# Layer 1's down phase: output rows on GpSimd's queue, other leads for loads and residual rows, weight sums from the third period

## The chip, the core and the metric

The kernel runs on one core of a Trainium2 chip. The metric is the device time of one execution in microseconds (us); the median of the runs counts. The core has a matrix engine (TensorE, PE in the profile), a vector engine (VectorE, DVE), an activation engine (ScalarE, ACT), GpSimd (POOL) and SyncE (SP), which only issues transfers. All of them run their own instructions in program order and wait for each other through semaphores. Transfers (DMA) between the main memory and the on-chip memory are issued here by SP and by POOL. PE writes its sums to banks (PSUM), from which VectorE and ScalarE read.

## What is computed

The reference is a small diffusion backbone with two layers over 1024 latent tokens of width 1024 and 256 context tokens. Each layer has attention and a feed-forward network with a short convolution, each followed by a residual sum and a layer norm:

```
        f_lat = conv_ffn(modulate(x_lat, m_lat[3], m_lat[4]), ffn_w_up[l], ffn_conv_w[l], ffn_conv_b[l], ffn_w_down[l])
        x_lat = layer_norm(DN_ALPHA * x_lat + m_lat[5] * f_lat, ln_g[l, 1], ln_b[l, 1])
...
def conv_ffn(h, w_up, conv_w, conv_b, w_down):
    u = h @ w_up
    L = u.shape[1]
    r = CONV_W // 2
    up = jnp.pad(u, ((0, 0), (r, r), (0, 0)))
    acc = conv_b
    for j in range(CONV_W):
        acc = acc + up[:, j:j + L] * conv_w[j]
    a, g = jnp.split(acc, 2, axis=-1)
    return (jax.nn.silu(g) * a) @ w_down
```

Here `w_up` is 1024 x 5632 and `w_down` 2816 x 1024. The second layer (number 1) returns only the latent rows, so its last layer norm gives the output: 1024 rows of 1024 floats.

## The kernel before

Everything is float32 at the boundary. For PE each operand is split in two parts, a rounded one (a cast on ScalarE) and the remainder (a subtraction on VectorE), and each block product is three matmuls. `split` (L101) does this for tiles of 128x512: the cast is L112, the subtraction L113.

The change lies in `ffn7` (L2070), layer 1's feed-forward network, and in `finish_o` in `run`, its last layer norm. Both matrix products there are done with seven block products in place of eight, with sums of blocks made beforehand. All engines run in the order in which the code is written (`manual_schedule`), so the place of a line in the program is its place in each engine's queue.

**Up phase.** 22 periods `p`, one for each pair of 128-column blocks of the up weights. Each has seven products on PE (L1691; 12 matmuls each). ScalarE copies banks and makes casts (L1663), VectorE subtracts and sums weights (L1665 to L1670), applies the convolution (L2149) and multiplies with the gate (L2181); the results and sums of them go to a buffer `G` in main memory through POOL's queue (L2155). The weights of period `p + 2` are loaded in period `p` (L1644).

Beside it runs the generator `side` = `mix_down` (L2037): for each of 11 rows of blocks of the down weights it loads four blocks of 128x512 on SP (L2046), makes four differences on VectorE (L2050) and stores them to a buffer `V` through POOL (L2051). It yields seven times a row, 77 times in all, and is advanced by `next(side, None)` at four places in each period. What is left is run after the last period. In the last period `load(0)` is issued near the start, and `load(1)` after it.

**Down phase.** 77 steps, 11 for each of seven products `q`; a step is 12 matmuls (L2350), three for each of four blocks of 128 rows. The sums lie in two groups of four banks, X and Y (`dx` and `dy` in the profile); `banks` says which product uses which. Between products ScalarE copies one group to the other (`copies`, L2390, after steps 10, 21, 43 and 65), and VectorE evicts finished banks to the rows `z` (`evict`: L2360 to L2365, also L2362 and L2363 where a saved part is added). `end` (L2371) finishes a row: statistics (L357 on VectorE, L359 and L360 on POOL), two passes over the row (L2809, L2812), and the store to the output (L2813 on SP).

`load(j)` (L2110) brings what steps 2j and 2j+1 need: a pair of weight blocks (from `V`, L2120, or from the down weights) and a pair from `G` (L2121), both 512 KB, on SP; then casts (L112 twice, L2129 for the `G` part) and subtractions (L113 twice, L2130). Each takes two of six raw buffers (`fr`), and of the split tiles there is room for six loads. Ahead of the steps of an even `i`, all loads up to `n` that were not yet issued are written: `n` is the step's own load plus a lead.

`job(i, ...)` hangs work behind step `i`: the loads of the residual rows z (L2394) and of the norm's and gate's rows, the scaling of the rows (`scale`, L2368 and L2369), `begin` (two rows for the last norm), the copies, evictions and ends. The jobs of rows 0 to 3 (`evict` with the saved part at steps 55, 57, 59, 61, `end` at 56, 58, 60, 62) fall between loads 33 to 36. The last nine steps run row block by row block: for each of the blocks 4 to 7 nine steps, then its eviction and its end.

Of the kernel before, what the change touches and what calls it, by code (L numbers as in the profile page):

```python
# [37 lines left out]
class Kern:  # L38
# [2031 lines left out]
    def ffn7(self, l, B, hps, T, dT, xsrc, gate_row, view, begin, finish, norm,  # L2070
# [3 lines left out]
        nc, io, d = self.nc, self.io, self.d  # L2074
# [5 lines left out]
        with ExitStack() as es:  # L2080
# [29 lines left out]
            def load(j):  # L2110

                s, m = 2 * j, min(2, 7 * HF - 2 * j)
                if m <= 0:
                    return
                r, g = raw(), raw()
                if m == 2 and (s + 1) % HF == 0:
                    nc.sync.dma_start(r[:, :1], right(s, 1))
                    nc.sync.dma_start(r[:, 1:], right(s + 1, 1))
                else:
                    nc.sync.dma_start(r[:, :m], right(s, m))  # L2120
                nc.sync.dma_start(g[:, :m], Gv[:, s : s + m])  # L2121
                for i, w in enumerate(self.split([r[:, i] for i in range(m)], 512)):
                    wd[s + i] = w
                if j < 3:
                    for i, w in enumerate(self.split([g[:, i] for i in range(m)], 512)):
                        ga[s + i] = w
                    return
                w = self.t(gp[0], [128, 2, 2, 512], "w", R)
                nc.scalar.copy(w[:, 0, :m], g[:, :m])  # L2129
                nc.vector.tensor_sub(w[:, 1, :m], g[:, :m], f32(w[:, 0, :m]))  # L2130
                for i in range(m):
                    ga[s + i] = w[:, :, i]

            side = self.mix_down(up, l)
# [80 lines left out]
            def get_T(m):  # L2215
                if m in more:
                    T[m], make[m] = self.load_T(tp, stage(m), dT, m, 0)

            def make_T(m, *which):
                if m in make:  # L2220
                    make[m](*which or range(3))

            c = none()
            late_l, YQ = None, {}

            def adds(Y, Q):


                for ps in (Y, Q):
                    nc.tensor.matmul(ps, ah[:, 0, :128], ah[:, 0], start=True, stop=True)  # L2230

            with self.tc.manual_schedule(engines=every):
                for m in range(4):
                    if m == 2 and 0 in make:
                        make_T(0)
                        make_T(1)
                    get_T(m)
                    for p in pre if m == 1 else []:
                        X, Y, Q = YQ[p] = (early["x", p],) + tuple(
                            self.t(pu, [128, 512], f"{x}{p}") for x in "yq"  # L2240
                        )
                        adds(Y, Q)
                        nc.scalar.copy(Y, X)
                        self.product(early[p][0][2], b21, X, False)
                for p in range(NP):
                    W2, call = [], lambda *x: None
                    if p == 0 and pre:
                        W2, call0 = early[1]
                        call = lambda what, i: i in (0, 2) or call0(what, i)
                    elif p + 1 < NP:  # L2250
                        W2, call = self.up_parts(raws)
                    if p in pre:
                        X, Y, Q = YQ[p]
                    else:
                        X = self.t(px or pu, [128, 512], f"x{p % 2}")
                        Y, Q = (self.t(pu, [128, 512], f"{x}{p % 2}") for x in "yq")
                    V = self.t(pu, [128, 512], f"v{p % 2}")
                    if p < 2 and p not in pre:
                        adds(Y, Q)
                    ua = self.t(up, [128, TLAT], "ua", bufs=2)  # L2260
                    ug = self.t(up, [128, TLAT], "ug")
                    u0, u1, v0, v1 = (view(u, h) for u in (ua, ug) for h in range(2))
                    if p not in pre:
                        self.product(W[0], (ah, al), X, True)
                    if late_l:
                        late_l("l", 5)
                        late_l("l", 6)
                    if p not in pre:
                        nc.scalar.copy(Y, X)
                    if p == NP - 1:  # L2270
                        load(0)
                    call("s", 1)
                    call("h", 0)
                    c.a1()
                    self.product(W[1], T[0], V, True)
                    if p + 2 < NP:
                        raws = self.up_raws(l, ORDER[p + 2])
                    nc.scalar.copy(u1, cols(V))
                    if p == 0:
                        make_T(2)  # L2280
                    call("h", 1)
                    c.g1()
                    call("l", 0)
                    c.a2()
                    next(side, None)
                    self.product(W[4], T[1], Y, False)
                    nc.scalar.copy(Q, Y)
                    if p == 0:
                        make_T(3)
                    call("h", 2)  # L2290
                    call("l", 1)
                    c.g2()
                    next(side, None)
                    if p not in pre:
                        self.product(W[2], b21, X, False)
                    nc.scalar.copy(u0, cols(X))
                    c.silu()
                    call("h", 3)
                    call("s", 4)
                    call("l", 2)  # L2300
                    self.product(W[5], T[2], Q, False)
                    call("h", 4)
                    call("l", 3)
                    c.store()
                    nc.vector.tensor_tensor(v1, u1, cols(Q), ALU.add)  # L2305
                    next(side, None)
                    self.product(W[6], b22, Y, False)
                    call("l", 4)
                    call("s", 5)
                    call("s", 6)  # L2310
                    nc.vector.tensor_tensor(u1, u1, cols(Y), ALU.add)
                    self.product(W[3], T[3], Q, False)
                    nc.scalar.copy(v0, cols(Q))
                    call("h", 5)
                    call("h", 6)
                    c.mix()
                    next(side, None)
                    c = conv(ua, ug, p)
                    W, late_l = W2, call
                for _ in side:  # L2320
                    pass
                load(1)
                for x in (c.a1, c.g1, c.a2, c.g2, c.silu, c.store, c.mix):
                    x()
# [3 lines left out]
        with ExitStack() as es, self.tc.manual_schedule(engines=every):  # L2328
            zp = es.enter_context(self.pool("fz"))
            gp[0] = es.enter_context(self.pool("fgs", bufs=6))  # L2330
            pd = es.enter_context(self.pool("fd", space=PSUM))
            z = [self.t(zp, [128, D], f"z{t}") for t in range(NLAT)]
# [43 lines left out]
            def job(i, f, *a):  # L2376
                jobs.setdefault(i, []).append(lambda: f(*a))
# [13 lines left out]

            job(3, start)
            for t in range(NLAT):
                job(6 + t, lambda t: nc.sync.dma_start(z[t], xsrc(t)), t)  # L2394
                job((18 + 2 * t) if t < 4 else (42 + 2 * (t - 4)), scale, t)
            job(16, alpha)
            job(28, begin, es, pd)
            job(HF - 1, copies, vs, Y)
            job(2 * HF - 1, copies, Y, X)
            job(4 * HF - 1, copies, X, Y)  # L2400
# [6 lines left out]
            ahead = 2  # L2407
            for i in range(NS - last):
                if i % 2 == 0:
                    n = i // 2 + min(5, 2 + i // 4)  # L2410
                    while ahead <= n:
                        load(ahead)
                        ahead += 1
                for t in range(4):
                    mm(i, t)
                for f in jobs.pop(i, ()):
                    f()
# [298 lines left out]
    def run(self):  # L2716
# [10 lines left out]
        nc, io, d = self.nc, self.io, self.d  # L2727
# [76 lines left out]
        def finish_o(t, z, s6):  # L2804
            st = box["st"]
            mv, rs = self.stats(st, s6)

            def norm_t():
                nc.vector.scalar_tensor_tensor(  # L2809
                    z, z, mv[:, 0:1], box["g"], ALU.subtract, ALU.mult  # L2810
                )
                nc.vector.scalar_tensor_tensor(z, z, rs, box["b"], ALU.mult, ALU.add)  # L2812
                nc.sync.dma_start(io["out"][t * 128 : (t + 1) * 128, :], z)  # L2813

            return norm_t, None

# [108 lines left out]
```

## Time and profile before

| what | us |
|---|---|
| median of three runs | 2955.36 |
| lowest and highest of them | 2953.01, 2955.71 |
| the profiled execution, its own time | 2951.48 |
| its span, from first to last instruction | 2949.7 |
| PE busy | 2771.6 (94%) |
| VectorE busy | 2118.9 (72%) |
| ScalarE busy | 1382.9 (47%) |
| POOL busy | 688.6 (23%) |
| up phase of layer 1, start to first matmul of the down phase | about 2245 to 2693.5 |
| down phase, first matmul to end of span | 2693.5 to 2949.7 |

The mean granted clock of TensorE is 0.975 of full speed. The page gives one profiled execution; its times count from the first instruction. A row of the timeline has start, length, engine, line, operation, output and input, the number of instructions merged, and in brackets the idle time of that engine before it and who ended it. A matmul in a row of them shows a longer time than it costs, as they overlap; what counts is the distance between starts.

### The profile page before, as it was taken

Reading aid. Unit: us, or ns where it says so; the run is one execution under the profiler, and the core shown is the slowest. Engines: PE = TensorE matmul, PEld = TensorE weight load, DVE = VectorE, ACT = ScalarE, POOL = GpSimd, SP = SyncE. Lnnn points to the kernel's source line nnn. Section 1 sums busy time; section 2 is a strip of 40 time slices with the busy share of each in tenths; the row PEclk is TensorE's granted clock in tenths of the full one; section 3 lists DMA queues with packets and bytes.
Section 4 is the critical chain, followed back from the end, with each engine's and each line's share of the span. In section 5 each row is a group of like instructions: output and inputs, shape, how many; then the busy total and the mean of one; then the engine's idle time right before and its main releaser. Section 6 shows DMA issues by size and latency. Waiting matters only on the chain.

```text
span 2949.7 us, 45178 instructions
## 1 busy us (share of the span) xinstructions
PE 2771.6 (94%) x16596; PEld 2256.5 (77%) x16596; DVE 2118.9 (72%) x3832; ACT 1382.9 (47%) x2597; POOL 688.6 (23%) x963
## 2 busy tenths in 40 slices
PE   7989899989999999999999978999998999999994
PEld 4877677777788988888888867766676788888783
DVE  4876366666578778888887566377766888887776
ACT  3311255567336655555553352177743555555531
POOL 2601133354450000000011023355542111110001
PEclk9999999999999999999999999999998999999997
DMA  8468711042667653343386436632154555556842
GB/s 261 145 189 278 221 37 35 9 153 76 170 182 224 201 161 108 111 118 113 93 321 221 141 106 220 192 87 69 48 164 149 161 178 168 172 168 216 299 146 85
DMA packets 370501, 456.87 MB, mean 155 GB/s; under 512 B 26136, under 2 KB 265016, under 8 KB 368744
## 3 DMA queue, kind: packets, MB, share of 16 engines
q1 hardware_dynamic: 343384, 371.50, 40.6%
q0 software_dynamic: 24000, 80.79, 8.0%
q8 instruction: 130, 2.13, 0.3%
q10 hardware_dynamic: 2896, 1.70, 0.2%
q14 instruction: 91, 0.75, 0.1%
HBM read 337.98 MB, written 115.93 MB: 154 GB/s over the span
## 4 chain that ended last, share of the span: by engine, by line
PE 68%; issue 9%; DMA 9%; DVE 8%; ACT 5%; POOL 1%; SPq 1%; ACTq 0%; DVEq 0%; POOLq 0%
PE x L1691 8%; PE q L1691 8%; PE y L1691 8%; PE S L762 5%; PE v L1691 4%; PE pv L907 3%; PE T L893 3%; PE dy L2350 3%; PE d L403 2%; PE d L402 2%; PE d L401 2%; PE mm L401 2%; PE mm L402 2%; PE mm L403 2%; PE pv L867 2%
## 5 line engine op out<-in xcount | busy, mean ns | idle before, releaser
L786 POOL TENSOR_SCALAR P<-P,rin 128x640 f32<-128x640 f32 (+3 forms) x288 | 249.5, 870 | 345.8 <-DVE rin L785 322.6
L112 ACT CAST w<-raw 128x512 fp32r<-128x512 f32 x315 | 183.0, 620 | 208.4 <-PE d L403 61.0
L1665 DVE TENSOR_TENSOR w<-raw,w 128x512 fp32r<-128x512 f32 x308 | 207.3, 687 | 84.1 <-ACT w L1663 84.0
L113 DVE TENSOR_TENSOR w<-raw,w 128x512 fp32r<-128x512 f32 x299 | 194.2, 689 | 92.7 <-ACT w L112 90.6
L762 PE MATMUL S<-k,q 64*128 64x256 f32 (+2 forms) x1824 | 192.2, 337 | 17.3 <-DVE nm L2639 8.0
L783 ACT ACTIVATE P<-P,nm 128x641 f32<-128x641 f32 (+4 forms) x208 | 161.4, 777 | 83.1 <-DVE nm L2639 46.1
L1663 ACT CAST w<-raw 128x512 fp32r<-128x512 f32 x308 | 182.0, 621 | 13.9 <-DVE raw L1670 7.8
L762 PEld LDWEIGHTS S<-k,q 64*128 64x128 f32 x1824 | 135.9, 188 | 52.8 <-issue 18.8
L773 ACT COPY PT<-T 128x512 f32<-128x512 f32 (+1 forms) x250 | 133.9, 565 | 77.6 <-PE T L893 75.6
L907 PE MATMUL pv<-PT,v 128*64 128x128 f32 x2016 | 132.4, 279 | 16.8 <-ACT PT L773 14.4
L2350 PE MATMUL dy<-w,w 128*128 128x512 f32 x528 | 122.7, 394 | 25.2 <-ACT dy L2390 25.2
L893 PE MATMUL T<-ident,P 128*128 128x128 f32 x1008 | 136.6, 282 | 7.6 <-POOL P L786 3.4
L907 PEld LDWEIGHTS pv<-PT,v 128*64 128x64 f32 x2016 | 108.5, 137 | 42.7 <-ACT PT L773 23.4
L401 PE MATMUL d<-w,w 128*128 128x512 f32 x352 | 138.6, 394 | 0.0
L403 PE MATMUL d<-w,w 128*128 128x512 f32 x352 | 138.0, 392 | 0.0
L402 PE MATMUL d<-w,w 128*128 128x512 f32 x352 | 138.0, 392 | 0.0
L2350 PEld LDWEIGHTS dy<-w,w 128*128 128x128 f32 x528 | 100.5, 191 | 47.1 <-ACT dy L2390 25.6
L771 DVE COPY PT<-T 128x512 f32<-128x512 f32 (+1 forms) x166 | 110.4, 666 | 31.3 <-PE T L893 21.1
L893 PEld LDWEIGHTS T<-ident,P 128*128 128x128 f32 x1008 | 110.2, 142 | 27.9 <-issue 14.1
L785 DVE RECIPROCAL rin<-den 128x1 f32<-128x1 f32 x288 | 46.0, 161 | 118.8 <-ACT P L783 116.2
L1691 PE MATMUL q<-T3h,w 128*128 128x512 f32 x352 | 118.2, 397 | 5.0 <-DVE ug L2305 4.2
L1691 PE MATMUL q<-T2h,w 128*128 128x512 f32 x352 | 115.9, 390 | 3.9 <-ACT q L1906 2.3
(416 smaller groups left out, 7814.0 us busy)
## 6 DMA issues: line engine op xcount, KB each, us to landing
raw<-in_up_dram SPq DMA_DIRECT2D x132, 512.0 KB
raw<-in_down_dram SPq DMA_DIRECT2D x59, 512.0 KB
raw<-g SPq DMA_DIRECT2D x44, 512.0 KB
raw<-G SPq DMA_DIRECT2D x38, 512.0 KB
araw<-in_ada_w_dram SPq DMA_DIRECT2D x32, 512.0 KB
raw<-in_w_in_dram SPq DMA_DIRECT2D x28, 512.0 KB
g<-cv POOLq DMA_DIRECT2D x22, 512.0 KB, 3.0
G<-go POOLq DMA_DIRECT2D x44, 256.0 KB, 2.7
```

Source lines behind the costliest of these rows:

```text
L112: nc.scalar.copy(hi, s)
L113: (lo_eng or nc.vector).tensor_sub(lo, s, f32(hi))
L401: nc.tensor.matmul(ps, lh, rh, start=first, stop=False)
L402: nc.tensor.matmul(ps, lh, rl, start=False, stop=False)
L403: nc.tensor.matmul(ps, ll, rh, start=False, stop=last)
L762: self.nc.tensor.matmul(outs[a], q[r, x, qs], k[r, y, ks], start=(i == 0), stop=(i == 2))
L786: nc.gpsimd.tensor_scalar(P[:, :n], P[:, :n], rin, 1.0, ALU.mult, ALU.mult)
L893: nc.tensor.transpose(ps[:, s * 128 : (s + 1) * 128], P[a][:, cols[i + x] : cols[i + x] + 128], self.ident,)
L907: nc.tensor.matmul(O[a * HD : (a + 1) * HD], v_of(a, vts[i + x]), pT[:, s * 128 : (s + 1) * 128], start=(i + x == 0), stop=(i + x == m - 1 ...
L1665: nc.vector.tensor_sub(half(i, 1), src[i], f32(half(i, 0)))
L1691: nc.tensor.matmul(ps, w[:, a, s], r[b][:, k], start=first and k + i == 0, stop=k == 3 and i == 2, skip_group_check=True,)
L2350: nc.tensor.matmul(banks[q][t], ga[i][:, a, c], wd[i][:, b], start=q < 2 and f + k == 0, stop=f == HF - 1 and k == 2, skip_group_check=True,)
```

## The change

Four things change.

- The stores of output rows 0 to 3 are issued by POOL; those of rows 4 to 7 stay on SP.
- The lead of the loads in the down phase grows more slowly: `i // 12` in place of `i // 4` is added to 2, up to 5. It is 2 up to step 10, 3 from 12, 4 from 24 and 5 from 36; before, it was 5 from step 12.
- The residual rows are loaded at steps 8, 11, ... 29 in place of 6 to 13, scaled at 20, 23, 26, 29 and 46 to 52 in place of 18 to 24 and 42 to 48, and `begin` moves from step 28 to 36.
- `side` is advanced only from the third period on (p > 1), so the 77 pieces run in periods 2 to 21 in place of 0 to 19.

```diff
+            def more_side(p):
+                if p > 1:
+                    next(side, None)
+
...
-                    next(side, None)
+                    more_side(p)
...
             for t in range(NLAT):
-                job(6 + t, lambda t: nc.sync.dma_start(z[t], xsrc(t)), t)
-                job((18 + 2 * t) if t < 4 else (42 + 2 * (t - 4)), scale, t)
+                job(8 + 3 * t, lambda t: nc.sync.dma_start(z[t], xsrc(t)), t)
+                job((20 + 3 * t) if t < 4 else (46 + 2 * (t - 4)), scale, t)
             job(16, alpha)
-            job(28, begin, es, pd)
+            job(36, begin, es, pd)
...
-                    n = i // 2 + min(5, 2 + i // 4)
+                    n = i // 2 + min(5, 2 + i // 12)
...
-                nc.sync.dma_start(io["out"][t * 128 : (t + 1) * 128, :], z)
+                q = nc.gpsimd if t < 4 else nc.sync
+                q.dma_start(io["out"][t * 128 : (t + 1) * 128, :], z)
```

The replacement of `next(side, None)` stands at all four places.

More of the change, by code (lines that the diff above doesn't have):

```diff
@@ L2292, in ffn7 @@
                     c.g2()
-                    next(side, None)
+                    more_side(p)
                     if p not in pre:
@@ L2305, in ffn7 @@
                     nc.vector.tensor_tensor(v1, u1, cols(Q), ALU.add)
-                    next(side, None)
+                    more_side(p)
                     self.product(W[6], b22, Y, False)
@@ L2316, in ffn7 @@
                     c.mix()
-                    next(side, None)
+                    more_side(p)
                     c = conv(ua, ug, p)
```

## The prediction

> **What bounds the kernel now.** I read the page first (PE is busy 94% of the span), then PE's timeline over the last 260 us, because the change sits in layer 1's feed-forward network and its down phase closes the program. The rows below are PE's, start, length, what, and in brackets the idle time before it with its releaser:
>
> ```profile
> 2723.77 30.08 PE L2350 MATMUL dx<-w,w 128*128 128x512 f32 x132
> 2757.58 32.78 PE L2350 MATMUL dx<-w,w 128*128 128x512 f32 x132 [3.73 <-ACT dy L2390]
> 2790.19 60.00 PE L2350 MATMUL dy<-w,w 128*128 128x512 f32 x264
> 2850.03 30.08 PE L2350 MATMUL dx<-w,w 128*128 128x512 f32 x132
> 2905.27 32.35 PE L2350 MATMUL dy<-w,w 128*128 128x512 f32 x132 [25.16 <-ACT dy L2390]
> ```
>
> A product of 11 steps (132 matmuls) takes (2850.03 - 2790.19) / 2 = 29.92 us, a step 2.72 us. PE stops twice, 3.73 and 25.16 us, both times for the copies between banks (L2390), and the product behind a stop is slower: 2790.19 - 2757.58 = 32.61 us and 32.35 us, so 2.7 and 2.4 us more. What makes the copy before the last product late? SP's rows and one of ACT:
>
> ```profile
> 2859.27 0.35 SPq L2813 DMA_DIRECT2D out_dram<-z  x1
> 2859.71 0.39 SPq L2120 DMA_DIRECT2D raw<-V  x1
> 2860.19 0.78 SPq L2121 DMA_DIRECT2D raw<-G  x1
> 2871.63 0.35 SPq L2813 DMA_DIRECT2D out_dram<-z  x1
> ```
> ```profile
> 2864.56 1.14 ACT L112 CAST w<-raw 128x512 fp32r<-128x512 f32 x2 [10.03 <-DMA raw<-V]
> ```
>
> The store of an output row stands on SP ahead of the next load and waits until VectorE has finished that row. The load leaves after it, lands 4.85 us after issue (2859.71 to 2864.56), is cast, and VectorE must subtract it before it may finish the next row. VectorE's rows:
>
> ```profile
> 2866.93 1.23 DVE L2130 TENSOR_TENSOR w<-raw,w 128x1024 fp32r<-128x1024 f32 x1 [0.43 <-ACT w L2129]
> 2868.08 0.20 DVE L357 BATCH_NORM_AGGREGATE mv<-s 128x2 f32<-128x12 f32 x1
> 2868.32 1.28 DVE L2809 SCALAR_TENSOR_TENSOR z<-z,mv,lg 128x1024 f32<-128x1024 f32 x1
> 2870.32 1.28 DVE L2812 SCALAR_TENSOR_TENSOR z<-z,rs,lb 128x1024 f32<-128x1024 f32 x1 [0.72 <-POOL rs L360]
> 2871.52 0.68 DVE L2362 TENSOR_TENSOR tt<-v,dy 128x512 f32<-128x512 f32 x1
> ```
>
> So store, load, cast, subtract, finish is a loop of 2871.63 - 2859.27 = 12.36 us, where two steps of PE take 5.44 us. Four turns eat the loads' lead and then 25 us. Engine share is not the limit there: waiting in SP's queue is.
>
> **The change part by part: the stores.** Four stores leave SP for POOL. SP then waits only for raw buffers (six, three loads' worth), freed by subtractions three loads back, so the loop is cut. What is late next? I lay VectorE's program order end to end from its first eviction of the sixth product, with these rows (an answer by line gives durations min/median/max, then first and last start):
>
> ```profile
> L2362 DVE TENSOR_TENSOR tt<-v,dy x4: 680/680/681, 2850.3 to 2884.1; 128x512 f32<-128x512 f32 x4
> L2362 DVE TENSOR_TENSOR tt<-v,dx x4: 669/672/680, 2908.5 to 2916.8; 128x512 f32<-128x512 f32 x4
> ```
> ```profile
> 2758.75 1.28 DVE L113 TENSOR_TENSOR w<-raw,w 128x512 fp32r<-128x512 f32 x2
> 2759.95 1.22 DVE L2130 TENSOR_TENSOR w<-raw,w 128x1024 fp32r<-128x1024 f32 x1
> 2761.09 1.22 DVE L2368 TENSOR_TENSOR z<-z,gb 128x1024 f32<-128x1024 f32 x1
> ```
> ```profile
> 2919.55 0.67 DVE L2360 TENSOR_TENSOR tt<-dy,gate 128x512 f32<-128x512 f32 x1
> ...
> 2923.95 1.28 DVE L2812 SCALAR_TENSOR_TENSOR z<-z,rs,lb 128x1024 f32<-128x1024 f32 x1 [0.71 <-POOL rs L360]
> ```
> ```profile
> L2812 DVE SCALAR_TENSOR_TENSOR z<-z,rs,lb x8: 1284/1284/1285, 2858.0 to 2942.1; 128x1024 f32<-128x1024 f32 x8
> ```
>
> An eviction with an addend: (2916.8 - 2908.5) / 3 = 2.77 us. A load's subtractions: 2761.09 - 2758.75 = 2.34. Finishing a row: 2871.52 - 2868.08 = 3.44. A row of the last product, evicted and finished: 2923.95 + 1.28 - 2919.55 = 5.68. From 2850.3 on, the order is four times evict, load, finish; then two loads, the last of half size (half of 2.34); four evictions; four last rows. That is 8 x 2.77 + 5 x 2.34 + 1.2 + 4 x 3.44 + 4 x 5.68 = 22.2 + 11.7 + 1.2 + 13.8 + 22.7 = 71.6 us, and 0.3 for ScalarE's cast, which the first load still follows: 71.9. Before, the same stretch lasts from 2850.3 to 2942.1 + 1.28 = 2943.4, so 93.1 us. **Gain 21.2 us.**
>
> PE alone would gain more. Its last product would start at 2850.03 + 29.92 = 2880.0, the rows of the last nine steps end every 6.12 us (27 matmuls) up to 2880.0 + 29.9 = 2909.9. VectorE reaches the last row only at 2850.3 + 71.9 - 5.7 = 2916.5, so in the tail **VectorE becomes the bound**, by 6.6 us. Does PE stay fed? In VectorE's order load 37 is subtracted at 2850.3 + 36.9 = 2887.2, and PE uses it from 2889.5 (two steps and 18 matmuls after 2880.0); the fourth bank is read out by 2850.3 + 0.3 + 3 x 8.55 + 0.7 = 2877.0, and its copy is due at about 2880. Both just hold, and a miss of 2 us there is paid out of PE's 6.6 us.
>
> On POOL the four stores stand between row statistics. Such a store was issued before, the x3 rows:
>
> ```profile
> L2690 POOL DMA_DIRECT2D x<-x x8: 587/613/627, 2170.2 to 2255.9; - x8
> ```
>
> It takes 0.61 us of POOL. Behind a waiting store stands only the next row's statistics, not due for 2.77 + 2.34 us, so I take nothing. Bounds: nothing, and 4 x 0.61 = 2.4 us if VectorE waited for each. No earlier store is waited for by anything but the end of the program.
>
> One rule speaks against this part. The Trainium skill (SBUF — State Buffer, "SBUF: two separate sides") says that a store from GpSimd's queue cannot get its descriptors written while VectorE runs an operation that uses both port pairs, and advises SP or ScalarE. The row agrees with no such delay (0.61 us with VectorE busy beside it), though other operations ran then; by the rule the sum would lose up to those 2.4 us.
>
> **Leads and residual rows.** ScalarE runs in order, so a bank copy waits for the casts of all loads put ahead of it. ScalarE's rows and one window (the columns are length, then PE, PEld, DVE, ACT and POOL busy, clock, DMA share, GB/s):
>
> ```profile
> 2750.59 1.05 ACT L2129 CAST w<-raw 128x1024 fp32r<-128x1024 f32 x1 [0.19 <-DMA raw<-G]
> ...
> 2755.99 1.04 ACT L2129 CAST w<-raw 128x1024 fp32r<-128x1024 f32 x1 [0.21 <-DMA raw<-G]
> 2756.95 2.04 ACT L2390 COPY dy<-dx 128x512 f32<-128x512 f32 x4
> ```
> ```profile
> 2715.00:2755.00 40.00, 38.85 (x172) 31.84 (x170) 24.32 (x31) 23.09 (x33) 0.00 (x0) 1.00 1.04 393
> ```
>
> The row at 2755.99 is load 15, that at 2750.59 load 13. DMA runs flat out at 393 GB/s. After step 21 the copies stand behind load 15 before; with i // 12 they stand behind load 13, and only four residual rows (of 512 KB, as the page's DMA issues say) go ahead of it on SP, not eight. Four rows less are 2.1 MB / 393 GB/s = 5.3 us, so load 13 is cast at about 2751.6 - 5.3 = 2746.3, before PE's first bank is done (2723.8 + 29.9 - 2.0 = 2751.6). The stop goes, and the slow product behind it: 66.42 - 59.84 = **6.6 us** (2723.77 to 2790.19, less two products). What is hidden: residual rows 4 to 7 load later, and their scaling moves from steps 42-48 to 46-52: two operations of 1.22 us beside a load's 2.34 in every 5.44 us, so VectorE has the room (4.8). Without that room the tail starts later by the overrun, about 2 us. Bounds: from nothing (copy still late) to 6.6.
>
> **Weight sums.** Periods 0 and 1 lose their loads and subtractions. PE's stop there (PE's row, then the piece of the chain) and two subtractions that stand ahead of its releaser:
>
> ```profile
> 2306.24 0.79 PE L1691 MATMUL q<-T3h,w 128*128 128x512 f32 x1 [3.58 <-DVE ug L2305]
> ```
> ```profile
> 2306.24 4.33 PE q L1691 x12
> ```
> ```profile
> L2050 DVE TENSOR_TENSOR va<-vb,va x1: 692/692/692, 2291.4 to 2291.4; 128x512 f32<-128x512 f32 x1
> L2050 DVE TENSOR_TENSOR vb<-vb,va x1: 684/684/684, 2297.0 to 2297.0; 128x512 f32<-128x512 f32 x1
> ```
>
> VectorE is late, and each subtraction is 0.6 us at its pace there. Following the order, an earlier one and the one at 2291.4 give about 0.6 together, since ScalarE's casts behind them bound the restart, and the third 0.6-0.7. **Gain 1.3 us**; bounds are nothing, and the stop with its slow product, 3.58 + 4.33 - 2.72 = 5.2.
>
> At the other end the sums now run to the last period, and load 0 stands behind their last load on SP. SP's rows of before (the same phase of the sums, two periods earlier; load 0) and ScalarE's cast of load 0:
>
> ```profile
> 2633.91 0.33 SPq L2046 DMA_DIRECT2D va<-in_down_dram  x1
> ...
> 2657.33 0.37 SPq L2120 DMA_DIRECT2D raw<-V  x1
> ```
> ```profile
> 2677.89 2.18 ACT L112 CAST w<-raw 128x512 fp32r<-128x512 f32 x4
> ```
>
> Two periods (of seven products of 12 matmuls, 19.04 us) later is 2672.0, so load 0 leaves at 2672.4 instead of 2657.33 and lands, at 4.85 us, at 2677.3: just in time for the cast at 2677.89. Cost nothing; up to 3 us if it lands late and the copies behind it hold PE.
>
> **Sum**: 21.2 + 6.6 + 1.3 = 29.1 us. The profiled execution took 2951.48 (its span 2949.7 and 1.8 around it), so it would take 2922.4. The median of the runs, 2955.36, lies 3.9 above that execution; the same gain from the median is **2926.3 us**.
>
> **The rivals.**
> - PE stays the bound of the tail (VectorE overlaps better than end to end): 2909.9 + 5.7 = 2915.6 against 2943.4, 27.8 instead of 21.2. Total 35.7, 2919.7 us. Against it: the rows above already follow each other without gaps. Chance 0.08.
> - The stop at step 21 stays, or load 0 lands late: the bytes are the same and DMA is full. Gain 22.5, 2932.9 us. For it: each margin is a few us. Chance 0.17.
> - GpSimd's stores wait for VectorE's pauses, and statistics behind them wait too: 2.4 us lost, 2928.7. Its ground is the row of 0.61 us, in an order where finish needs POOL. Chance 0.05. (The skill's rule above would be the cause.)
> - The change doesn't do what it says: loads stay tied to VectorE's row finishing although SP is free, as raw buffers come free behind it. Then only the issue gap of 0.44 us per turn goes, 1.8 in all; with 6.6 and 1.3 that is 9.7, 2945.7 us. Against it: three loads can be in flight. Chance 0.04.
> - Slower: the small lead starves PE in the first 24 steps, where three loads at most stand ahead of it. It decides when a load's round, from issue to subtracted, exceeds 3 x 5.44 = 16.3 us. At 25 us, 16 loads would lose 25 / 3 - 5.44 = 2.9 us each, 46 us; less 29 that is 17 us slower, 2972 us. Against it: SP's issue is tied to buffers and not to steps, and a round now (4.85 landing, 1.14 + 1.05 casts, 2.34) is near 10 us. Chance 0.03.
>
> **How the numbers follow.** The forecast has 0.63. Its own bounds run from 2919 to 2935; with the rivals at 2919.7 and 2932.9, and a few us for the spread of the runs, the range is 2916 to 2940; outside lie the two last rivals and some of the spread. A measurement of this kernel can tell about 0.2% (6 us) from no change. Faster by over that: 0.95 (all but the last, and a remainder of 0.02 within it); slower 0.03.
>
> **What would show it.** Step by step: no idle row before L2350's last product, and none at 2757; SP's L2813 rows only four; VectorE without gaps from the sixth product to the end, and PE ending some 12 us before the last row is finished instead of 6; load 0's cast at the old place in the last period. A PE wait at step 21, a cast of load 0 that waits for DMA, POOL stores well over 0.61 us with statistics waiting, or VectorE idle in the tail would prove the steps wrong one by one.

## The result, and the profile after

The changed kernel takes **2927.18 us** (median of four runs, 2925.49 to 2932.86) against 2954.53 us for the kernel before on the same chip: a ratio of 0.9911, with an interval of 0.9894 to 0.9928. That is 27.4 us less. The forecast was 2926.3 us from a base of 2955.36, 29.1 us less. The profiled execution took 2927.96 us, with a span of 2926.1.

The lines of the changed program stand four further down, or five for the store: L2350 is now L2354, the second pass over a row L2816, the store L2818. First PE's rows in the down phase (start, length, operation, and idle time before it with its releaser):

```profile
2696.62 11.81 PE L2354 MATMUL dy<-w,w 128*128 128x512 f32 x50
2709.06 18.88 PE L2354 MATMUL dy<-w,w 128*128 128x512 f32 x82 [0.63 <-DVE w L113]
2727.78 60.00 PE L2354 MATMUL dx<-w,w 128*128 128x512 f32 x264
2787.62 60.00 PE L2354 MATMUL dy<-w,w 128*128 128x512 f32 x264
2847.46 30.08 PE L2354 MATMUL dx<-w,w 128*128 128x512 f32 x132
2877.38 30.08 PE L2354 MATMUL dy<-w,w 128*128 128x512 f32 x132
```

Both stops at bank copies are gone, and no product is slow: 2787.62 - 2727.78 = 59.84 us for two, 29.92 each. In their place stands one wait of 0.63 us in the first product. Now SP's rows in the tail:

```profile
2860.67 0.36 SPq L2120 DMA_DIRECT2D raw<-V  x1
2861.80 0.36 SPq L2121 DMA_DIRECT2D raw<-G  x1
2869.23 0.33 SPq L2120 DMA_DIRECT2D raw<-V  x1
2870.36 0.33 SPq L2121 DMA_DIRECT2D raw<-G  x1
2902.63 17.19 SPq L2818 DMA_DIRECT2D out_dram<-z  x4
```

The last loads leave without a store between them; SP's four stores come 32 us later. The other four are POOL's. The answer for the line of the store gives durations in ns, then first and last start, and how long a POOL store took to land:

```profile
L2818 POOL DMA_DIRECT2D out_dram<-z x4: 583/590/594, 2857.0 to 2882.7; - x4
...
DMA to landing us min/median/max: 2.9/2.9/3.3
```

VectorE, at the place where the loop was read in the kernel before, and its first and last instruction of the tail:

```profile
2860.56 1.22 DVE L2130 TENSOR_TENSOR w<-raw,w 128x1024 fp32r<-128x1024 f32 x1
2861.69 0.20 DVE L357 BATCH_NORM_AGGREGATE mv<-s 128x2 f32<-128x12 f32 x1
2861.93 1.29 DVE L2813 SCALAR_TENSOR_TENSOR z<-z,mv,lg 128x1024 f32<-128x1024 f32 x1
2863.95 1.29 DVE L2816 SCALAR_TENSOR_TENSOR z<-z,rs,lb 128x1024 f32<-128x1024 f32 x1 [0.73 <-POOL rs L360]
2865.15 0.68 DVE L2366 TENSOR_TENSOR tt<-v,dy 128x512 f32<-128x512 f32 x1
```
```profile
2847.69 0.68 DVE L2366 TENSOR_TENSOR tt<-v,dy 128x512 f32<-128x512 f32 x1
...
2918.18 1.29 DVE L2816 SCALAR_TENSOR_TENSOR z<-z,rs,lb 128x1024 f32<-128x1024 f32 x1 [0.72 <-POOL rs L360]
```

The subtraction no longer waits for a cast (no bracket at L2130, where 0.43 us and before it a DMA stood). From the first eviction of the sixth product to the end of the last row VectorE needs 2919.47 - 2847.69 = 71.8 us, where 71.9 was forecast and 93.1 stood before. It is not without gaps in it: eight waits of 0.72 or 0.73 us for POOL's statistics, 5.8 us in all, lie inside the 3.44 and 5.68 us that the prediction took for a row. PE ends at about 2907.3, 12.2 us ahead of it.

To see where all the time went, I cut layer 1's feed-forward network at PE's rows: A from the first matmul of the up phase to that of the third period, B to the first of the down phase, C to the start of its fourth product, D from there to the end of the last row. The same cuts, in us, serve for every run below:

| kernel | A | B | C | D | sum |
|---|---|---|---|---|---|
| before | 64.9 | 383.1 | 96.7 | 153.2 | 697.9 |
| changed | 62.2 | 384.5 | 91.0 | 131.8 | 669.5 |
| changed, another execution | 64.1 | 385.5 | 91.1 | 131.9 | 672.6 |
| stores only | 64.3 | 383.3 | 95.6 | 131.8 | 675.0 |
| leads and rows only | 66.0 | 383.6 | 90.1 | 154.4 | 694.0 |
| sums only | 62.2 | 384.2 | 93.0 | 152.7 | 692.1 |
| stores late on SP | 62.2 | 385.3 | 90.1 | 131.8 | 669.4 |
| old lead | 62.3 | 384.8 | 91.0 | 131.8 | 670.0 |
| old rows | 62.2 | 385.5 | 91.4 | 131.8 | 671.0 |
| sums from the first period | 64.6 | 383.5 | 90.1 | 131.8 | 670.0 |
| sums from the second | 62.2 | 383.8 | 90.1 | 131.8 | 667.9 |
| saved part early | 64.0 | 386.8 | 90.1 | 126.8 | 667.7 |
| saved part early, sums from the second | 62.2 | 384.4 | 90.1 | 126.8 | 663.5 |
| the same, Silu's table early | 63.0 | 383.8 | 90.1 | 126.8 | 663.6 |

The sum falls by 28.4 us from before to changed. The span falls by only 23.6, because the changed kernel's profiled execution reached this network 4.5 us later (2249.95 against 2245.47 us), through code that is the same in both. That start lay between 2244.3 and 2254.4 in the thirteen profiled executions after the first, which is why the stages tell more than whole times where a few us are asked for.

### The profile page after: what moved, and what is told of

Read it like the earlier page. It is cut to its first block, busy times and chain, and to the rows that moved or that the text cites. A ratio compares the mean times of both kernels' runs of the same rounds, so it can differ in the third digit from the quotient of the medians.

```text
span 2926.1 us, 45178 instructions
## 1 busy us (share of the span) xinstructions
PE 2765.7 (95%) x16596; PEld 2254.8 (77%) x16596; DVE 2117.6 (72%) x3832; ACT 1383.0 (47%) x2597; POOL 691.5 (24%) x967
## 4 chain that ended last, share of the span: by engine, by line
PE 68%; issue 10%; DVE 9%; DMA 6%; ACT 5%; POOL 1%; SPq 0%; ACTq 0%; DVEq 0%; POOLq 0%
PE q L1691 8%; PE x L1691 8%; PE y L1691 7%; PE S L762 4%; PE v L1691 4%; PE pv L907 3%; PE T L893 3%; PE dy L2354 3%; PE mm L401 2%; PE d L402 2%; PE d L403 2%; PE d L401 2%; PE mm L402 2%; PE mm L403 2%; PE dx L2354 2%
## 5 line engine op out<-in xcount | busy, mean ns | idle before, releaser
L2354 PE MATMUL dy<-w,w 128*128 128x512 f32 x528 | 120.8, 390 | 0.6 <-DVE w L113 0.6
L2643 DVE CUSTOM_DVE_ANT_0 P<-S,msk,snk 128x640 f32<-128x640 f32 (+1 forms) x128 | 103.7, 846 | 16.9 <-PE S L762 13.5
```

The lines of the kernel that those rows point to most:

```text
L2354: nc.tensor.matmul(banks[q][t], ga[i][:, a, c], wd[i][:, b], start=q < 2 and f + k == 0, stop=f == HF - 1 and k == 2, skip_group_check=True,)
```

## The experiments

**One part at a time.** The theory was that the four stores' place on SP is worth the tail, the leads and rows the stop at step 21, the sums next to nothing. First the stores alone, in the kernel before:

```diff
-                nc.sync.dma_start(io["out"][t * 128 : (t + 1) * 128, :], z)
+                q = nc.gpsimd if t < 4 else nc.sync
+                q.dma_start(io["out"][t * 128 : (t + 1) * 128, :], z)
```

> The kernel before, with only the four stores moved to GpSimd's queue. Theory (the stores' wait on SP cuts the loads, and behind it VectorE's own work is the bound): no PE idle before the last product; from the first eviction of the sixth product VectorE's chain lasts 71.9 us instead of 93.1, so the time falls by 21 us; the stop of PE at step 21 stays (3.7 us, and 2.7 us of slower matmuls behind it). Rival 1 (PE is the bound of the tail): 27.8 us less. Rival 2 (the lead of the loads and the spread of the rows are needed too): the idle time before the last product stays at 10 us or more, and less than 15 us is gained.

2933.73 against 2953.34 us, ratio 0.9926 (0.9907 to 0.9945). PE's rows of this kernel:

```profile
2761.87 31.75 PE L2350 MATMUL dx<-w,w 128*128 128x512 f32 x132 [3.67 <-ACT dy L2390]
2793.47 60.00 PE L2350 MATMUL dy<-w,w 128*128 128x512 f32 x264
2853.31 30.08 PE L2350 MATMUL dx<-w,w 128*128 128x512 f32 x132
2883.23 30.08 PE L2350 MATMUL dy<-w,w 128*128 128x512 f32 x132
```

The stop at step 21 is there, the one before the last product is not. D falls from 153.2 to 131.8 by the stores alone, so neither lead nor rows are needed for it, and the 27.8 us of a tail bound by PE did not come.

Then only the leads, rows, scaling and `begin`:

```diff
-                job(6 + t, lambda t: nc.sync.dma_start(z[t], xsrc(t)), t)
-                job((18 + 2 * t) if t < 4 else (42 + 2 * (t - 4)), scale, t)
+                job(8 + 3 * t, lambda t: nc.sync.dma_start(z[t], xsrc(t)), t)
+                job((20 + 3 * t) if t < 4 else (46 + 2 * (t - 4)), scale, t)
...
-            job(28, begin, es, pd)
+            job(36, begin, es, pd)
...
-                    n = i // 2 + min(5, 2 + i // 4)
+                    n = i // 2 + min(5, 2 + i // 12)
```

> The kernel before, with only the lead of the loads, the residual rows, their scaling and the last norm's rows as in the changed kernel. Theory: the stop at step 21 goes with the slow product behind it, and everything after it comes 6.6 us earlier; the loop of stores and loads on SP stays, with some 25 us of PE idle before the last product. Time 6 to 7 us less. Rival 1: the late rows and scaling run into the store loop and give it back (0 us). Rival 2: the lead matters to the store loop (more than 10 us).

2948.54 us, ratio 0.9977 (0.9967 to 0.9987), which is 6.8 us of 2953, while the medians lie 4.8 us apart. C falls by 6.6, but D is 1.2 longer, so in the stages not all of it arrives at the end (A, which nothing of the edit reaches, is 1.1 longer besides); the store loop stays, as PE's row says:

```profile
2902.90 32.58 PE L2350 MATMUL dy<-w,w 128*128 128x512 f32 x132 [26.17 <-ACT dy L2390]
```

And only the sums (the second of these lines, at all four places):

```diff
-                    next(side, None)
+                    more_side(p)
```

> The kernel before, with only the weight sums from the third period on. Theory, from the trace of the changed kernel: 2.7 us gained from the first two periods, 1.3 us lost in the last period, where load 0 lands late, and up to 0.9 us in the first product of the down phase: 0 to 1.5 us less in sum, no difference that can be told. Rival: the first two periods are the whole of it (1.3 us forecast, 2.7 us at most) and nothing is lost at the end.

2952.23 us, ratio 0.9991 (0.9981 to 1.0001): no difference that can be told. A is 2.7 shorter and B 1.1 longer. C is shorter too, since the stop at step 21 is only 2.60 us here and the product behind it nearly normal (next start 2783.76, so 30.07 us); that this comes from the sums is not shown, as nothing of the edit reaches there.

```profile
2753.69 30.23 PE L2354 MATMUL dx<-w,w 128*128 128x512 f32 x132 [2.60 <-ACT dy L2394]
```

**Queue or order?** The stores went to another queue, but they could as well have gone to a later place on the same one:

```diff
+            job(6 * HF + 1, rows_out)
...
-                q = nc.gpsimd if t < 4 else nc.sync
-                q.dma_start(io["out"][t * 128 : (t + 1) * 128, :], z)
+                o = io["out"][t * 128 : (t + 1) * 128, :]
+                if t < 4:
+                    box.setdefault("late", []).append((o, z))
+                else:
+                    nc.sync.dma_start(o, z)
...
+        def rows_out():
+            for o, z in box["late"]:
+                nc.sync.dma_start(o, z)
```

> The changed kernel, with the four stores back on SP, but written behind the last load (step 67) instead of behind each row. Theory (it is the order on SP that costs, not which queue carries the store): the time of the changed kernel within 2 us. Rival (GpSimd's queue itself brings the gain, or costs something): more than 3 us away from it.

2927.05 us, ratio 0.9900 (0.9885 to 0.9914), and D is 131.8 again. What counts is that no load stands behind a store; GpSimd's queue is one way to that.

**Lead or rows?** The changed kernel with one of the two undone, `i // 4` or the old places of rows, scaling and `begin`:

```diff
-                    n = i // 2 + min(5, 2 + i // 12)
+                    n = i // 2 + min(5, 2 + i // 4)
```

> The changed kernel with the old lead (i // 4). Theory (ScalarE's copies wait for the casts of the loads ahead of them, and DMA sets these): with four residual rows less ahead of it, load 15 is cast by 2752.8 in the clock of the kernel before, and the copy that PE waits for can start until about 2753.2: no stop at step 21, or one under 1 us; time within 2 us of the changed kernel. Rival (the lead is what removes the stop): 3.7 us of PE idle and 2.7 us of slower matmuls come back.

```diff
-                job(8 + 3 * t, lambda t: nc.sync.dma_start(z[t], xsrc(t)), t)
-                job((20 + 3 * t) if t < 4 else (46 + 2 * (t - 4)), scale, t)
+                job(6 + t, lambda t: nc.sync.dma_start(z[t], xsrc(t)), t)
+                job((18 + 2 * t) if t < 4 else (42 + 2 * (t - 4)), scale, t)
...
-            job(36, begin, es, pd)
+            job(28, begin, es, pd)
```

> The changed kernel with the old places of the residual rows, their scaling and the last norm's rows. Theory: the copies after step 21 stand behind load 13, which was cast at 2751.6 in the kernel before with all eight rows ahead of it, so no stop at step 21, or one under 1 us; time within 2 us of the changed kernel. Rival (the spread of the rows is what removes the stop): some 6.5 us come back.

2925.66 us (0.9907, 0.9894 to 0.9921) and 2925.41 us (0.9907, 0.9894 to 0.9921): neither can be told from the changed kernel. PE's rows of the two, first that with the old lead, run through step 21 without a stop:

```profile
2723.14 60.00 PE L2354 MATMUL dx<-w,w 128*128 128x512 f32 x264
```
```profile
2728.92 60.00 PE L2354 MATMUL dx<-w,w 128*128 128x512 f32 x264
```

Each edit alone removes the stop; together they do it twice. The stop was 3.7 us, and by the rows before each takes about 5 us out of what stands ahead of the copy: 2755.99 - 2750.59 = 5.4 us from load 13 to load 15, and an estimated 5.3 us for four residual rows.

**When to start the sums.** In the changed kernel the sums' last load stands ahead of load 0 on SP. SP's rows, then ScalarE's casts of load 0 and PE's row:

```profile
2674.00 0.33 SPq L2046 DMA_DIRECT2D va<-in_down_dram  x1
2674.42 0.77 SPq L2120 DMA_DIRECT2D raw<-V  x1
2675.29 1.48 SPq L2121 DMA_DIRECT2D raw<-G  x1
```
```profile
2681.30 1.14 ACT L112 CAST w<-raw 128x512 fp32r<-128x512 f32 x2 [1.49 <-DMA raw<-V]
2682.61 1.14 ACT L112 CAST w<-raw 128x512 fp32r<-128x512 f32 x2 [0.17 <-DMA raw<-G]
```
```profile
2693.73 0.50 PE L1691 MATMUL q<-T3h,w 128*128 128x512 f32 x1 [0.88 <-DVE ug L2309]
```

It leaves at the forecast place (2672.4 and 1.8 us of shift), but is cast 6.9 us after its issue instead of 4.85. ScalarE waits 1.49 us, and PE 0.88 us in the last period and 0.63 us in the first product. Two kernels move the start:

```diff
             def more_side(p):
-                if p > 1:
+                if p > -1:
```

> The changed kernel with the weight sums from the first period on again. Theory: load 0 leaves before the last period again, ScalarE's casts of it do not wait for DMA, and PE's idle time in the last period (0.9 us) and in the first product (0.6 us) goes; the stop in the second period gets longer by 0.6 us and another 0.6 us comes back. Time within 1.5 us of the changed kernel. Rival (the later start is worth 2.7 us without a price): 2 to 3 us slower.

```diff
             def more_side(p):
-                if p > 1:
+                if p > 0:
```

> The changed kernel with the weight sums from the second period on. Theory: the last of their loads stands one period earlier on SP, so load 0 leaves and lands in time and the stops in the last period and the first product go (2.2 us), while the second period has one subtraction more ahead of PE's releaser (0.6 us): 1 to 2 us faster than the changed kernel. Rival (load 0 is late for another reason): the stops stay, and the time is the same or 0.6 us longer.

2926.95 us (0.9911, 0.9897 to 0.9925) and 2924.22 us (0.9910, 0.9894 to 0.9926). In both, load 0 is in time; ScalarE's row of the first of them has no wait, and PE's of the second no break in the first product:

```profile
2677.74 2.19 ACT L112 CAST w<-raw 128x512 fp32r<-128x512 f32 x4
```
```profile
2693.88 30.39 PE L2354 MATMUL dy<-w,w 128*128 128x512 f32 x132
```

B and C together are 473.6 and 473.9 us, where the changed kernel has 475.5 and 476.7 in two executions: the late load costs about 1.6 to 3.1 us. The start in the second period keeps A as well (62.2, with the same stop of 2.98 us), where 0.6 us was expected to come back; in whole times the two can't be told from the changed kernel.

**What bounds the tail now.** If it is VectorE's own work, less of it must show:

```diff
-                job((20 + 3 * t) if t < 4 else (46 + 2 * (t - 4)), scale, t)
+                job((20 + 3 * t) if t < 4 else (42 + 3 * (t - 4)), scale, t)
+                job((20 + 3 * t) if t < 4 else (42 + 3 * (t - 4)), fold, t)
...
+            def gated(t):
+                nc.vector.tensor_mul(vs[t], vs[t], gate[:, 512:])
+
+            def fold(t):
+                nc.vector.tensor_add(z[t][:, 512:], z[t][:, 512:], vs[t % 4])
...
-                job(5 * HF + 2 * t, evict, t, 1, Y[t], vs[t])
+                job(HF + 2 + t, gated, t)
+                job(5 * HF + 2 * t, evict, t, 1, Y[t])
...
-                job(6 * HF + t // 2, evict, 4 + t, 1, X[t], vs[t])
+                job(6 * HF + t // 2, evict, 4 + t, 1, X[t])
```

> The changed kernel, with the saved part of the second column half multiplied by the gate and added to the rows early (16 operations less than 0.7 us each, 4 + 8 of them at steps 13 to 51, where VectorE has room), so that the eight evictions of the tail have three operations instead of four. Theory (VectorE's own work is the bound of the tail, PE has 6.6 us to spare): 8 x 0.61 = 4.9 us less than the changed kernel. Rival (PE, the loads or the stores bound the tail): no change.

(The text's 16 operations should read 12, as its own count of 4 + 8 says.) An eviction of the tail now has three operations, in VectorE's rows:

```profile
2864.22 0.68 DVE L2364 TENSOR_TENSOR tt<-dy,gate 128x512 f32<-128x512 f32 x1
2864.94 0.69 DVE L2368 TENSOR_TENSOR z<-z,tt 128x512 f32<-128x512 f32 x1
```

D falls from 131.8 to 126.8, by 5.0 us where 4.9 was expected, and C doesn't pay for it (90.1). So VectorE's program order is shown to be the bound. In whole times it is not told apart: 2925.65 us, ratio 0.9903 (0.9886 to 0.9919), beside the changed kernel's 2927.55 and 0.9913 (0.9898 to 0.9928) in the same series; the profiled execution had a stop of 2.1 us in the middle of the up phase (in B) that the edit doesn't touch. What the changed kernel was expected to show in that series:

> The changed kernel itself, beside the next two on the same chip: 0.991 of the kernel before by either theory.

With the sums from the second period besides:

> The same, with the weight sums from the second period on. Theory: both gains add, 6 to 7 us less than the changed kernel. Rival: only the 4.9 us of the tail, or nothing.

2920.73 us, ratio 0.9888 (0.9873 to 0.9902): 6.8 us below the changed kernel, as expected. The intervals of the two ratios still touch, but the four times (2916.80 to 2922.22) all lie below the four of the changed kernel beside them (2925.41 to 2929.62).

**What holds PE in the second period.** PE still stops there for 2.98 us, in the changed kernel's row:

```profile
2307.71 0.61 PE L1691 MATMUL q<-T3h,w 128*128 128x512 f32 x1 [2.98 <-DVE ug L2309]
```

Silu's table load was taken out of the chain by an early Silu, in the kernel with the saved part early and the sums from the second period:

```diff
+                    if p == 0:
+                        nc.scalar.activation(ua[:, 512:528], self.mhalf, AF.Silu)
                     nc.scalar.copy(u1, cols(V))
```

> The kernel with the saved part added early and the weight sums from the second period on, and besides a Silu of 16 columns on ScalarE in the first period, while it waits for PE, so that the load of Silu's table (1.28 us, in the second period behind VectorE's convolution) is done by then. Theory (the stop of PE in the second period is held by the chain convolution, table, Silu, cast, subtraction, product, sum, so taking VectorE's subtractions out shortens it by little): the stop falls from 3.0 to 1.7 us, and the slow matmuls behind it (4.6 us for 12 instead of 2.72) go if the clock holds, so 1.3 to 3.2 us less from the up phase's first to its third period. Rival 1 (VectorE's load holds the stop): it stays at 3.0 us. Rival 2 (ScalarE's copies and casts in between bring the old table back): a second load of 1.28 us appears, and the time is the same or longer.

PE's row, and the group of the table load in the answer by lines (busy us, mean ns, idle before):

```profile
2304.67 0.50 PE L1691 MATMUL q<-T3h,w 128*128 128x512 f32 x1 [2.16 <-DVE ug L2311]
```
```profile
L2283 ACT ACT_TABLE_LOAD x1 | 1.3, 1283 | 0.0
```

There is one table load, off the chain, and the stop is 0.8 us shorter, so the chain through ScalarE did hold it; not by the full 1.28 us, since VectorE's own order is next, with 0.35 us of waiting for a load of the weight sums and 0.6 us for their subtraction in front of the sum that PE waits for. The matmuls behind the stop stay slow (4.27 us from the first of 12 to the next product). Against the expectation, A is not 1.3 to 3.2 us shorter but 0.8 longer (63.0 against 62.2): PE's clock was halved for 20.1 us of it instead of 13.7. 2917.17 us, ratio 0.9879 (0.9863 to 0.9896), is the lowest median of all, but the stages add up to about the same as those of the kernel before it in the table (663.6 and 663.5), so no gain of the early Silu is shown. Both versions are faster than the kernel before by intervals that leave out 1; that this one beats the changed kernel, which was not measured beside it, is not shown.

## Why the prediction was right

- **The store loop** was the 25 us stop. The gain of the tail was 21.2 us forecast, 21.3 measured (D), and the stores alone bring it.
- **VectorE as the next bound** decided the size. Reading only PE's stop and the slow product behind it would have given 27.6 us. The sum of VectorE's program order, 71.9 us against 71.8, gave the right one, and 5.0 us come back when work leaves it. Margins of PE held: no idle row in the tail.
- **The price of GpSimd's queue** was taken as nothing; the stores took 0.59 us of POOL, and the kernel with them late on SP has the same D. The rule of the Trainium skill (SBUF — State Buffer, "SBUF: two separate sides") would by the prediction have cost up to 2.4 us. These traces show none of it: the stores land in 2.9 us (3.3 at most) with VectorE busy for 36.2 of the 40 us around them, on two-input operations and passes; an operation that the rule names for both port pairs, such as a float32 copy, did not run there, so the rule itself was not put to the test.
- **The stop at step 21**: 6.6 us forecast, and C falls by 6.6 where only the leads and rows are changed. In the changed kernel it falls by 5.7, as the late load 0 costs 0.9 in the first product. The two edits were treated as one sum; the runs show that either is enough.
- **The weight sums** are the step that failed, in its term for the other end: "Cost nothing; up to 3 us if it lands late". The landing was taken from a quieter place (4.85 us) and is 6.9 us here, where one more load and four stores of 256 KB each were issued within 2.1 us before it, and with longer issues (0.77 and 1.48 us on SP). The price is 1.6 to 3.1 us, about the upper bound that the prediction gave. At the start the size was right: PE's waits for VectorE fall by 1.2 us (the stop from 3.58 to 2.98, and one of 0.61 us in the first period is gone) where 1.3 was forecast. (The upper bound of 5.2 us there took 4.33 us for 12 matmuls up to the end of the last; from start to start it is 4.16, so 5.0.) A shows 2.7 in the profiled execution and 0.8 in another of the same kernel (64.1), because PE's clock was halved for 13.7 us of A in the one, and for 20.5 in the other as in the kernel before. Together the part is worth nothing that can be told.

In sum: 21.3 + 5.7 + 2.7 - 1.3 (B) = 28.4 us in the profiled stages, 27.4 in the medians, 29.1 forecast. That the sum comes so near is in part luck: the price of the late load, 2.2 us in B and C that the forecast left out, is made up for the most part by the 1.5 us (2.7 - 1.2) that A gained through the clock in this one execution.

## What to carry to other kernels

A store that waits for results should not stand ahead of loads on one queue: it ties the loads to the engine that makes the results, and a lead of several loads is eaten turn by turn. Before putting a price on such a stop, lay the next engine's program order end to end; here that second bound took 6 us of the gain. When two edits aim at one wait, undo each alone: one may be enough.

## What was not expected of the hardware

The time lost behind a stop of PE did not follow the stop's length. Stops of 3.73 and 3.67 us at step 21 were followed by 2.7 and 1.7 us of extra time in the product, one of 2.60 us by 0.15 us. But in the second period of the up phase stops of 2.98 and 2.16 us were followed by 1.7 and 1.55 us for 12 matmuls (4.44 and 4.27 us from start to start instead of 2.72). The Trainium skill (TensorE: Matmul & The Clock Gate, "What's actually happening") has the clock halved after an idle window of about 3.4 us whose phase is free. The granted clock of these traces agrees with the window: in each execution it changes only at whole multiples of 3.41 us from its first change, so stretches at half clock last 3.41 us, 6.83 us and so on. But the traces show that a window need not be idle throughout. The stop of 2.16 us lay within one window (2302.49 to 2305.91 us), and the clock was 0.50 in the next; so it was for the stop of 2.98 us (2304.53 to 2307.94). The stop of 2.60 us fell on two windows, with 1.79 us without a matmul in one and 0.81 in the other, and the clock stayed at 1.00.

In all fourteen traces, from 2235 to 2910 us, every window at full clock with 2.00 us or more without a matmul is followed by half clock, and none with 1.92 us or less; the full clock returns after a window with 0.62 us or less without a matmul, and not with 0.69 or more. These bounds are read from this stretch alone: earlier in the program the clock was also halved after a window with only 1.31 us (changed kernel, at 1912.0). So what a short stop costs depends on where it falls among the windows, and that place differs from one execution to the next.
